# A hybrid S5 and RG-LRU layer on one core: the branch b projection in seven products per pair of blocks, and the C load in front of the S5 recurrence

## The chip, the cores and the metric

The kernel runs on one core of one Trainium2 chip. The metric is the device time of one execution in microseconds, as a median over executions. The core has a matrix engine (PE; its weight loads are listed as PEld), a vector engine (DVE), a scalar engine (ACT), GpSimd (POOL), and a sync engine (SP) which issues all DMA of this kernel.

## What is computed

One layer of a decoder trunk, for a prompt of 512 tokens and 8 sample sequences of 4 tokens, 544 tokens in all, with 2048 channels. Cut to what matters here:

```python
proj = xn @ p["w_in"] + p["b_in"]
u_a, z_a, x_b, z_b, g_a, g_b = jnp.split(proj, _SPLITS, axis=-1)
y_a, s5_re, s5_im = _s5_branch(u_a, s5_re0, s5_im0, p)
y_b, rg_h, conv_buf = _rglru_branch(x_b, rg_h0, conv0, p)
y_a = y_a * jax.nn.silu(z_a)
y_b = y_b * jax.nn.silu(z_b)
merged = (jax.nn.sigmoid(g_a) * (y_a @ p["w_proj_a"])
          + jax.nn.sigmoid(g_b) * (y_b @ p["w_proj_b"]))
out = merged @ p["w_out"]
x = x + gate[:, None] * out
```

The S5 branch is a complex diagonal recurrence h over the tokens in 64 groups of 64 states, with y = Re(C h) + D u, a GELU and a GLU. `w_proj_b` is 2048 x 2048, `w_proj_a` 1024 x 2048. All is float32.

## The kernel before

A float32 product is made of three matmuls on a rounded format: a value x is kept as hi = round(x) and lo = x - hi, and hi·xh, hi·xl and lo·xh are summed in PSUM. Activations lie with channels on the 128 partitions and tokens along the free dimension: 16 blocks of 128 channels by 544 tokens (T), two halves of 272 (HT), since a PSUM bank takes 512 values. `split_x` (176) makes xh on ACT and xl on DVE for one such block. `weights` (151) loads a raw tile of 1 MB (2048 values on each partition; three buffers) and `split_w` (137) makes hi on ACT (144) and lo on DVE (145), 1024 values each, four buffers each. `product` (165) makes one block of 128 output channels: with 16 blocks of k it issues 96 matmuls of 272 columns (line 172), with 8 blocks 48.

The stages follow one another: the ada vectors; the input projection in 80 blocks (u, z_a, the gates g_a and g_b, later x_b and z_b), beside which the S5 branch runs; the RG-LRU; the GLU of branch a (961 to 969); the a projection (974 to 984); the b projection (989 to 1000); w_out (1010 to 1063).

S5 steps are hung between the blocks of the input projection by a list, `spread` (lines 722 to 728) and `beside`: `s5_far` (powers of the transition), `s5_near`, `s5_over` and `s5_into` are the recurrence, all on DVE in `rotated` (five operations, with tiles v and t, on the state tile eh, whose neighbours along the recurrence lie eight values apart). `s5_c` loads C in four tiles r (649), transposes each on PE into q (653) and copies it by ACT to cp and cq. `s5_y1` makes ca from cp and cq and then the first matmuls of the output, pk (664). The r tiles and the recurrence's v and t share one tag with three buffers:

```python
def t2k(shape, name):
    return p1.tile(shape, F32, tag="t2k", name=name, bufs=3)
```

In the GLU, y of block j is multiplied and split into ah, al. The a projection loads gad (the gate, line 974), applies a sigmoid (976), multiplies it with the product on DVE and stores it to pad (981); beside it, ybd (the RG-LRU's output) comes back block by block and is split into bh, bl (984). The b projection loads gbd and pad, multiplies and adds on DVE (helper `tt`, line 403), and splits the merged blocks for w_out. Tiles loaded with `loaded` (800) share four buffers, tag ld.

Which instruction stands where on each engine is set by the Tile scheduler, which lays the program out by a timeline of its own; each engine then works through its list in order and waits on semaphores.

Of the kernel before, what the change touches and what calls it, by code (L numbers as in the profile page):

```python
# [9 lines left out]
F32 = mybir.dt.float32  # L10
F32R = mybir.dt.float32r
# [8 lines left out]
P = 128  # L20
# [3 lines left out]
T = TP + NS * TS  # L24
# [31 lines left out]
def tile_hybrid_s5_rglru(  # L56
# [137 lines left out]
    MC = 72  # L194
    cs = const.tile([P, KD, MC], F32R, name="cs")
    cv_ = pt[:, :KD * 9].rearrange("p (k b) -> p k b", b=9)
# [3 lines left out]

    shift = const.tile([P, KD, 9], F32, name="shift")
    gmul = const.tile([P, KD, 9], F32, name="gmul")
    gate = const.tile([P, KD, 9], F32, name="gate")
# [90 lines left out]
    def columns(pieces, name):  # L294
        t = p0.tile([P, P], F32, tag="rows", name="rows", bufs=2)
        if sum(b - a for a, b, _ in pieces) < P:
            pool.memset(t, 0.0)
        for a, b, src in pieces:
            dq2.dma_start(t[a:b], src)
        pt = aux_tile("pt")  # L300
        pe.transpose(pt[:, :P], t, ident)
        o = const.tile([P, P], F32, name=name)
        act.activation(o, pt[:, :P], AF.Copy)
        return o
# [409 lines left out]
    for q in range(16):  # L714
# [237 lines left out]

    st2.close()


# [14 lines left out]

    bh, bl = [None] * KD, [None] * KD
    for j in range(16):
        if j % 2 == 0:
            wts = weights(w_proj_a[0], j * P, 8)
        sg = loaded(gad, j, p3)
# [10 lines left out]
    mh, ml, mm = [None] * KD, [None] * KD, [None] * KD  # L986
    for j in range(16):
        sg, m_ = loaded(gbd, j, p3), p3.tile([P, T], F32, tag="mm", name="mm", bufs=8)
        dq2.dma_start(m_, pad[j])
        act.activation(sg, sg, AF.Sigmoid)  # L990
        acc = product(weights(w_proj_b[0], j * P, KD), 0, KD, bh, bl)
        for h in range(2):
            sl = slice(h * HT, (h + 1) * HT)
            tt(dve, sg[:, sl], acc[h][:, :HT], sg[:, sl], MUL)
        tt(dve, m_, m_, sg, ADD)
        mm[j] = m_
        if j < 8:
            split_x(m_, j, mh, ml)
    for j in range(8, 16):
        split_x(mm[j], j, mh, ml)  # L1000
    st3.close()
# [8 lines left out]
    for t0, t1 in ((256, T), (0, 256)):  # L1010
# [10 lines left out]
        done = 0  # L1021
        for j in range(KD):
            wts = weights(w_out[0], j * P, KD)
            acc = acc_tile("acc")
            for k in range(KD):
                h, l = wts(0, k)
                for w_, x_, first, last in ((h, mh, k == 0, False), (h, ml, False, False),
                                            (l, mh, False, k == KD - 1)):
                    pe.matmul(acc[:, :t1 - t0], lhsT=w_, rhs=x_[k][:, t0:t1], start=first, stop=last)  # L1029
            og = p4.tile([P, T - 256], F32, tag="og", name="og", bufs=3)  # L1030
            np_ = min(t1, TP) - t0
# [65 lines left out]
```

## Time and profile before

| what | us |
|---|---|
| runs, median of 3 | 1831.95 |
| lowest, highest | 1820.18, 1832.62 |
| the profiled execution | 1823.58 |
| its span in the profile | 1821.8 |
| PE busy, share of the span | 1749.4, 96% |
| DVE busy | 928.4, 51% |
| ACT busy | 737.5, 40% |

Durations come from that one profiled execution. The chain of waits is followed back from the last instruction, at each step to what released it; the share of an engine in it is time that counted. Windows give the busy time of each engine within a stretch, and the granted clock of PE (1.00 is 2.4 GHz, 0.50 is 1.2 GHz).

### The profile page before, as it was taken

Reading aid. Unit: us, or ns where it says so; the run is one execution under the profiler, and the core shown is the slowest. Engines: PE = TensorE matmul, PEld = TensorE weight load, DVE = VectorE, ACT = ScalarE, POOL = GpSimd, SP = SyncE. Lnnn points to the kernel's source line nnn. Section 1 sums busy time; section 2 is a strip of 40 time slices with the busy share of each in tenths; the row PEclk is TensorE's granted clock in tenths of the full one; section 3 lists DMA queues with packets and bytes.
Section 4 is the critical chain, followed back from the end, with each engine's and each line's share of the span. In section 5 each row is a group of like instructions: output and inputs, shape, how many; then the busy total and the mean of one; then the engine's idle time right before and its main releaser. Section 6 shows DMA issues by size and latency. Waiting matters only on the chain.

```text
span 1821.8 us, 32528 instructions
## 1 busy us (share of the span) xinstructions
PE 1749.4 (96%) x13420; PEld 1687.4 (93%) x13420; DVE 928.4 (51%) x1394; ACT 737.5 (40%) x1134; POOL 148.1 (8%) x385
## 2 busy tenths in 40 slices
PE   7889999999599999999999999999999999999997
PEld 4558999999599999999999999999999999999997
DVE  4795255548863233224556565655543433355654
ACT  7864232332122222223555545555333322134543
POOL 2100000000000000010222122321000000000000
PEclk9989999999799999999999999999999999999999
DMA  9887435442335545444444453542776644376682
GB/s 323 278 281 188 127 97 135 111 117 74 106 104 140 143 115 145 122 134 122 128 134 134 113 167 119 159 145 93 222 253 211 185 136 123 105 222 178 175 224 94
DMA packets 400278, 281.56 MB, mean 155 GB/s; under 512 B 68513, under 2 KB 350457, under 8 KB 398905
## 3 DMA queue, kind: packets, MB, share of 16 engines
q1 hardware_dynamic: 400130, 279.49, 53.1%
q8 instruction: 105, 1.72, 0.4%
q14 instruction: 43, 0.35, 0.1%
HBM read 244.64 MB, written 32.44 MB: 152 GB/s over the span
## 4 chain that ended last, share of the span: by engine, by line
PE 78%; DVE 7%; DMA 7%; ACT 4%; issue 2%; SPq 2%; POOL 0%; ACTq 0%; DVEq 0%; POOLq 0%
PE acc L172 58%; PE acc L1029 11%; DVE lo L145 2%; DMA raw<-in_w_in_dram 2%; PE pg L881 1%; DVE t L403 1%; PE gacc L821 1%; PE ada L218 1%; SPq L675 1%; DVE v L403 1%; DMA xt<-in_x_prompt_dram 1%; DMA ybd<-zb 1%; ACT hi L144 1%; PE pk L664 1%; DMA raw<-in_w_ada_dram 1%
## 5 line engine op out<-in xcount | busy, mean ns | idle before, releaser
L145 DVE TENSOR_TENSOR lo<-raw,hi 128x1024 fp32r<-128x1024 f32 x374 | 455.1, 1222 | 559.6 <-ACT hi L144 541.9
L172 PE MATMUL acc<-xh,hi 128*128 128x272 f32 x3424 | 718.2, 290 | 4.9 <-ACT adasb L228 2.6
L172 PE MATMUL acc<-xh,lo 128*128 128x272 f32 x3424 | 717.7, 289 | 1.2 <-DVE lo L145 1.2
L172 PE MATMUL acc<-xl,hi 128*128 128x272 f32 x3424 | 717.1, 289 | 0.0
L144 ACT ACTIVATE hi<-raw 128x1024 fp32r<-128x1024 f32 x374 | 391.1, 1056 | 674.3 <-PE acc L172 541.9
L172 PEld LDWEIGHTS acc<-xh,hi 128*128 128x128 f32 x3424 | 541.3, 189 | 10.8 <-ACT adasb L228 3.1
L172 PEld LDWEIGHTS acc<-xh,lo 128*128 128x128 f32 x3424 | 539.5, 189 | 2.5 <-DVE lo L145 1.7
L172 PEld LDWEIGHTS acc<-xl,hi 128*128 128x128 f32 x3424 | 540.6, 189 | 0.9 <-DVE xl L181 0.2
L1029 PE MATMUL acc<-xl,hi 128*128 128x288 f32 (+1 forms) x512 | 149.3, 292 | 0.0
L1029 PE MATMUL acc<-xh,hi 128*128 128x288 f32 (+1 forms) x512 | 148.6, 291 | 0.0
L1029 PE MATMUL acc<-xh,lo 128*128 128x288 f32 (+1 forms) x512 | 147.3, 288 | 0.0
L1029 PEld LDWEIGHTS acc<-xh,lo 128*128 128x128 f32 x512 | 96.6, 189 | 0.1
L1029 PEld LDWEIGHTS acc<-xl,hi 128*128 128x128 f32 x512 | 96.5, 188 | 0.3
L1029 PEld LDWEIGHTS acc<-xh,hi 128*128 128x128 f32 x512 | 96.2, 188 | 0.1
L403 DVE TENSOR_TENSOR ld<-acc,ld 128x272 f32<-128x272 f32 x64 | 25.2, 434 | 53.1 <-PE acc L172 53.1
L218 PE MATMUL ada<-lo,cs 128*72 128x512 f32 x128 | 45.0, 436 | 7.3 <-DVE lo L145 6.5
L218 PE MATMUL ada<-hi,cs 128*72 128x512 f32 x128 | 44.3, 430 | 7.5 <-ACT hi L144 7.1
L765 ACT ACTIVATE r<-pg,c 128x284 f32<-128x284 f32 x64 | 29.7, 492 | 39.7 <-PE pg L881 39.7
L181 DVE TENSOR_TENSOR xl<-ld,xh 128x544 fp32r<-128x544 f32 x24 | 17.3, 723 | 50.8 <-ACT xh L179 50.7
L856 DVE SCALAR_TENSOR_TENSOR cv<-xb,c,cv 128x568 f32<-128x568 f32 x48 | 38.8, 809 | 1.5
L218 PEld LDWEIGHTS ada<-hi,cs 128*72 128x72 f32 x128 | 18.6, 154 | 22.0 <-ACT hi L144 11.1
L218 PEld LDWEIGHTS ada<-lo,cs 128*72 128x72 f32 x128 | 16.7, 151 | 21.1 <-DVE lo L145 16.9
(311 smaller groups left out, 1416.2 us busy)
## 6 DMA issues: line engine op xcount, KB each, us to landing
raw<-in_w_in_dram SPq DMA_DIRECT2D x80, 1024.0 KB
raw<-in_w_ada_dram SPq DMA_DIRECT2D x64, 512.0 KB
raw<-in_w_out_dram SPq DMA_DIRECT2D x32, 1024.0 KB
raw<-in_w_ada_dram SPq DMA_DIRECT2D x16, 1024.0 KB
raw<-in_w_proj_b_dram SPq DMA_DIRECT2D x16, 1024.0 KB
raw<-in_w_proj_a_dram SPq DMA_DIRECT2D x8, 1024.0 KB
u<-ud SPq DMA_DIRECT2D x128, 41.0 KB
gad<-sg SPq DMA_DIRECT2D x16, 272.0 KB
```

The lines of the kernel that those rows point to most:

```text
L144: act.activation(hv, src, AF.Copy)
L145: dve.tensor_tensor(out=lv, in0=src, in1=hv, op=SUB)
L172: pe.matmul(acc[j][:, :HT], lhsT=w_, rhs=x_[k][:, j * HT:(j + 1) * HT], start=first, stop=last)
L218: pe.matmul(accs[i][:MC], lhsT=cs[:, k, :], rhs=w_[:, i * 512:(i + 1) * 512], start=first, stop=last)
L403: eng.tensor_tensor(out=out, in0=a, in1=b, op=op)
L664: pe.matmul(pk[:GC, i * P:(i + 1) * P], lhsT=bb[:, 4 * q + i], rhs=ca[:, i, 0:8].rearrange("p j c -> p (j c)"), start=True, stop=True)
L675: dq2.dma_start(m4[GC * (7 - s):GC * (8 - s), :, GC * s:], k4[:, :, 0:P - GC * s])
L765: turn[0] = act.activation(*args, **kw)
L821: pe.matmul(gacc[0][:MC], lhsT=cs[:, k0 + k, :], rhs=w_[:, k % 2 * 512:(k % 2 + 1) * 512], start=first, stop=last)
L856: dve.scalar_tensor_tensor(out=cv, in0=xb[:, k:k + FT], scalar=convw_c[:, k * 16 + j:k * 16 + j + 1], in1=cv, op0=MUL, op1=ADD)
L881: pe.matmul(pg[:, :FH], lhsT=w_[:, g], rhs=x_[:, sl], start=first, stop=last)
L1029: pe.matmul(acc[:, :t1 - t0], lhsT=w_, rhs=x_[k][:, t0:t1], start=first, stop=last)
```

## The change

Two parts.

The b projection takes output blocks in pairs. A weight matrix part of 2048 x 256 is cut into four quarters: even and odd blocks of k, and the first and second 128 columns (`quarters`); the activations likewise into even and odd blocks of channels and the two halves of the tokens. Strassen's scheme in Winograd's form then needs seven products of a quarter by a quarter (24 matmuls of 272 columns each) instead of eight. The seven weight operands are made one after the other by four differences on DVE, in place in the raw tiles, and split each into hi and lo (`seven_weights`). The seven activation operands a0, s1, s2, b0, s3, s4, b1 (for 8 block pairs each) are made during the a projection by `build` and `build_late`, and ybd is no longer split as it stands. Three PSUM banks a, e, b collect the products; partial results are copied by ACT and added by DVE. The merged block goes back to pad, and blocks 0 to 11 are loaded again and split during the last pair. The first two blocks of w_out are started together with k 0 to 11, and get k 12 to 15 afterwards. Constants needed only early move to a pool `early` that ends before, to make room.

The C load `s5_c` is hung in front of `s5_far`, not in the third of the four blocks that carry the recurrence.

```diff
+    def set_sums(f, a, b, eng):
+        a0, a1, b0, b1 = a[:, :HT], a[:, HT:], b[:, :HT], b[:, HT:]
+        s1, s2, s3, s4 = f
+        eng.tensor_tensor(out=s1, in0=a1, in1=b1, op=ADD)
+        eng.tensor_tensor(out=s2, in0=s1, in1=a0, op=SUB)
+        eng.tensor_tensor(out=s4, in0=b0, in1=s2, op=SUB)
+        eng.tensor_tensor(out=s3, in0=a0, in1=a1, op=SUB)
+        return {"a0": a0, "a1": a1, "b0": b0, "b1": b1, "s1": s1, "s2": s2, "s3": s3, "s4": s4}
+
+    def split_half(src, room):
+        act.activation(room[:, 0], src, AF.Copy)
+        dve.tensor_tensor(out=room[:, 1], in0=src, in1=room[:, 0], op=SUB)
+
+    def quarters(w, col):
+        out = []
+        for s in range(2):
+            raw = raw_tile()
+            dq.dma_start(raw.rearrange("p (i m) -> p i m", i=8),
+                         w[:, col:col + 256].rearrange("(i s p) m -> s p i m", s=2, p=P)[s])
+            v = raw.rearrange("p (i h m) -> p h i m", i=8, h=2)
+            out += [v[:, 0], v[:, 1]]
+        return out
+
+    ORDER = ("a0", "s1", "s2", "b0", "s3", "s4", "b1")
+
+    def seven_weights(w, col):
+        b11, b12, b21, b22 = quarters(w, col)
+        def sub(o, x, y):
+            dve.tensor_tensor(out=o, in0=x, in1=y, op=SUB)
+            return o
+        yield split_w(b11)
+        yield split_w(sub(b11, b12, b11))
+        yield split_w(sub(b11, b22, b11))
+        yield split_w(b21)
+        yield split_w(sub(b12, b22, b12))
+        yield split_w(b22)
+        yield split_w(sub(b21, b21, b11))
...
+    def seven(head, sets, left, right, bias=(None, None)):
+        g, wt = head
+        wt = wt + list(g)
+        a, e, b = (acc_tile(f"acc{x}")[:, :HT] for x in "aeb")
+        def run(n, bank, new, done):
+            for i in range(8):
+                h, l = (v[:, i * P:(i + 1) * P] for v in wt[n])
+                xh_, xl_ = sets[ORDER[n], i]
+                for w_, x_, f, z in ((h, xh_, i == 0, False), (h, xl_, False, False), (l, xh_, False, i == 7)):
+                    pe.matmul(bank, lhsT=w_, rhs=x_, start=new and f, stop=done and z, skip_group_check=True)
...
+        run(0, a, True, True)
+        run(1, e, True, True)
+        out(l0, a, bias[0])
+        out(r1, e, bias[1])
+        run(2, a, False, True)
+        out(r0, a, bias[1])
+        run(3, b, True, True)
+        dve.tensor_tensor(out=l0, in0=l0, in1=b, op=ADD)
+        run(4, a, False, True)
+        dve.tensor_tensor(out=r1, in0=r1, in1=a, op=ADD)
+        run(5, e, False, True)
+        dve.tensor_tensor(out=r0, in0=r0, in1=e, op=ADD)
+        run(6, a, False, True)
+        out(l1, a, bias[0])
...
-    spread([s5_far] + [lambda i=i: s5_near(i) for i in range(1, 8)]
+    spread([s5_c, s5_far] + [lambda i=i: s5_near(i) for i in range(1, 8)]
            + [lambda c=c, f=f: f(c) for c in range(1, 8) for f in (s5_over, s5_into)], 10, 14)
-    spread([s5_c], 12, 13)
...
+    def build(i):
+        fa = p3.tile([P, 2, HT], F32, tag="fa", name="fa")
+        fb = p3.tile([P, 2, HT], F32, tag="fb", name="fb", bufs=4)
+        v = set_sums([fa[:, 0], fa[:, 1], fb[:, 0], fb[:, 1]],
+                     loaded(ybd, 2 * i, p3), loaded(ybd, 2 * i + 1, p3), dve)
+        kept[i] = v
+        for n in ORDER if i < 4 else ORDER[:3]:
+            split_half(v[n], room[n, i])
...
-        split_x(loaded(ybd, j, p3), j, bh, bl, xpool if j < 8 else px)
...
+        if j % 2 == 0:
+            coming = weights(w_proj_a[0], (j + 2) * P, 8) if j < 14 else seven_head(w_proj_b[0], 0, 4)
+        if j in (0, 2, 4, 6, 7, 9, 11, 13):
+            build(len(kept))
+    head = coming
+    for n in ORDER[3:]:
+        build_late(n)
...
+    for j0 in range(0, 16, 2):
+        cs_ = [wk.tile([P, T], F32, tag=t_, name="c", bufs=2) for t_ in ("z", "sg")]
+        seven(head, sets, *cs_)
+        if j0 < 14:
+            head = seven_head(w_proj_b[0], (j0 + 2) * P)
+        else:
+            head = weights(w_out[0], 0, KD)
+            for j in range(12):
+                split_x(loaded(pad, j, p3), j, mh, ml)
+        for j, c in zip((j0, j0 + 1), cs_):
+            sg, m_ = loaded(gbd, j, p3), loaded(pad, j, p3)
+            act.activation(sg, sg, AF.Sigmoid)
+            tt(dve, c, c, sg, MUL)
+            tt(dve, c, c, m_, ADD)
+            merged[j] = c
+            if j < 12:
+                dq2.dma_start(pad[j], c)
+    for j in range(12, 16):
+        split_x(merged[j], j, mh, ml)
```

Where the instructions stand. Counted along PE's list, the four groups of C transposes now stand behind 2035, 2047, 2064 and 2098 matmuls of line 172, formerly behind 2499 to 2533, and the first pk behind 2623, formerly 2649. The last matmuls of `s5_e` (pw, line 569) stand behind 2027 in both.

DVE at the end of `s5_far` before, up to the recurrence's first operation v:

```order
L403 TENSOR_TENSOR q2_4037<-q1_4036,q2_4037 128x256
L403 TENSOR_TENSOR t_4060<-q2_4037,q1_4036 128x256
L145 TENSOR_TENSOR lo_4592<-raw_4585,hi_4591 128x1024
L403 TENSOR_TENSOR q1_4036<-q1_4036,t_4056 128x256
L403 TENSOR_TENSOR q2_4037<-q2_4037,t_4060 128x256
L403 TENSOR_TENSOR v_4064<-eh_1434,q1_4036 128x512
L403 TENSOR_TENSOR t_4065<-eh_1434,q2_4037 64x512 x2
```

The same place after (t_5159 is a product with cq, the transposed C):

```order
L487 TENSOR_TENSOR t_4097<-q2_4078 128x256
L487 TENSOR_TENSOR q2_4078<-q1_4077,q2_4078 128x256
L487 TENSOR_TENSOR t_4101<-q2_4078,q1_4077 128x256
L487 TENSOR_TENSOR t_5159<-a2_1439,cq_4058 128x576
L487 TENSOR_TENSOR q1_4077<-q1_4077,t_4097 128x256
L487 TENSOR_TENSOR q2_4078<-q2_4078,t_4101 128x256
L487 TENSOR_TENSOR v_4105<-eh_1437,q1_4077 128x512
```

The first product with cq has moved in front of the recurrence, and the t tiles take buffers that the r tiles of C had just before.

ACT at the change from the GLU (line 965 before, 1049 after) to the a projection before; ld of line 976 is the gate gad, xh of line 179 the split of y:

```order
L144 ACTIVATE hi_14043<-raw_14037 128x1024
L965 ACTIVATE sg_13894<-acc0_13844,c1_224 128x272
L965 ACTIVATE sg_13894<-acc1_13845,c1_224 128x272
L976 ACTIVATE ld_13975<-ld_13975 128x544
L179 ACTIVATE xh_13899<-ld_13840 128x544
L179 ACTIVATE xh_13971<-ld_13969 128x544
L144 ACTIVATE hi_14173<-raw_14171 128x1024
```

The same place after; xset are the operands of `build(0)`, fa holds s1 and s2, fb s3 and s4, ld_14025 and ld_14027 are ybd blocks:

```order
L146 ACTIVATE hi_14019<-raw_14013 128x1024
L1049 ACTIVATE sg_13898<-acc0_13848,c1_227 128x272
L1049 ACTIVATE sg_13898<-acc1_13849,c1_227 128x272
L198 ACTIVATE xset_13907<-fa_14023 128x272
L198 ACTIVATE xset_13911<-fa_14023 128x272
L198 ACTIVATE xset_13915<-ld_14027 128x272
L198 ACTIVATE xset_13919<-fb_14024 128x272
L181 ACTIVATE xh_13903<-ld_13844 128x544
L198 ACTIVATE xset_13923<-fb_14024 128x272
L198 ACTIVATE xset_13927<-ld_14027 128x272
L198 ACTIVATE xset_13931<-ld_14025 128x272
```

The last split of y (xh_13903, before xh_13899) now stands behind four copies of build(0), and the gate's sigmoid behind it.

DVE in the b projection before, one block of 128 channels and part of the next:

```order
L403 TENSOR_TENSOR mm_15125<-mm_15125,ld_15123 128x544
L145 TENSOR_TENSOR lo_15375<-raw_15368,hi_15374 128x1024
L181 TENSOR_TENSOR xl_15241<-mm_15125,xh_15239 128x544
L145 TENSOR_TENSOR lo_15491<-raw_15488,hi_15490 128x1024
L403 TENSOR_TENSOR ld_15243<-acc0_15258,ld_15243 128x272
L403 TENSOR_TENSOR ld_15243<-acc1_15259,ld_15243 128x272
L403 TENSOR_TENSOR mm_15245<-mm_15245,ld_15243 128x544
```

DVE there after, most of one pair; line 219 is a difference of weights, line 262 and 264 (not in this piece) the additions from PSUM:

```order
L487 TENSOR_TENSOR c_15653<-c_15653,ld_15876 128x544
L147 TENSOR_TENSOR lo_15865<-raw_15855,hi_15864 128x1024
L487 TENSOR_TENSOR c_15653<-c_15653,ld_15878 128x544
L219 TENSOR_TENSOR raw_15855<-raw_15857,raw_15855 128x8x128
L147 TENSOR_TENSOR lo_15888<-raw_15855,hi_15887 128x1024
L147 TENSOR_TENSOR lo_15892<-raw_15857,hi_15891 128x1024
L487 TENSOR_TENSOR c_15652<-c_15652,ld_15868 128x544
L147 TENSOR_TENSOR lo_15897<-raw_15855,hi_15896 128x1024
L219 TENSOR_TENSOR raw_15857<-raw_15857,raw_15855 128x8x128
L487 TENSOR_TENSOR c_15652<-c_15652,ld_15870 128x544
L147 TENSOR_TENSOR lo_15901<-raw_15857,hi_15900 128x1024
L147 TENSOR_TENSOR lo_15906<-raw_15857,hi_15905 128x1024
```

The differences stand between the lo of the products, in the order in which the seven products need them.

## Rows read from the trace of the kernel before

**Rows 1.** The page: busy time, and the chain by line.
```profile
PE 1749.4 (96%) x13420; PEld 1687.4 (93%) x13420; DVE 928.4 (51%) x1394; ACT 737.5 (40%) x1134; POOL 148.1 (8%) x385
...
PE acc L172 58%; PE acc L1029 11%; DVE lo L145 2%; DMA raw<-in_w_in_dram 2%; PE pg L881 1%; DVE t L403 1%; PE gacc L821 1%; PE ada L218 1%; SPq L675 1%; DVE v L403 1%; DMA xt<-in_x_prompt_dram 1%; DMA ybd<-zb 1%; ACT hi L144 1%; PE pk L664 1%; DMA raw<-in_w_ada_dram 1%
```

**Rows 2.** Windows: length, busy PE, PEld, DVE, ACT, POOL, clock, DMA share, GB/s.
```profile
1330.00:1418.00 88.00, 88.00 (x699) 88.00 (x698) 33.09 (x53) 30.68 (x45) 0.00 (x0) 1.00 0.72 223
1415.00:1608.00 193.00, 193.00 (x1526) 193.00 (x1525) 74.19 (x99) 55.35 (x66) 0.00 (x0) 1.00 0.47 131
1608.00:1640.00 32.00, 32.00 (x245) 31.88 (x245) 15.02 (x26) 11.66 (x14) 0.15 (x2) 1.00 0.92 286
```

**Rows 3.** Waits: engine, line, releaser, us in total, times, longest.
```profile
PE q L653 <- DMA r<-in_s_c_im_dram: 18.4, 1, 18.4
...
PE acc L172 <- ACT xh L179: 2.3, 1, 2.3
...
DVE v L403 <- PE q L653: 6.7, 1, 6.7
...
DVE t L403 <- PE q L653: 1.8, 1, 1.8
```

**Rows 4.** Chain of waits: start, us, what; from three stretches.
```profile
417.99 12.08 PE acc L172 x96
...
1279.80 8.27 DMA raw<-in_w_proj_a_dram
...
1318.11 2.76 DMA ld<-gad
...
1320.97 0.66 ACT ld L976
1321.63 0.55 ACT xh L179
...
1322.23 24.29 PE acc L172 x190
```

**Rows 5.** Lines by form, DVE and ACT in 1420:1600; the last row DVE in 1322:1414.
```profile
L145 DVE TENSOR_TENSOR lo<-raw,hi 128x1024 fp32r<-128x1024 f32 x31 | 37.8, 1222 | 68.1 <-ACT hi L144 68.1
L403 DVE TENSOR_TENSOR ld<-acc,ld 128x272 f32<-128x272 f32 x31 | 12.2, 435 | 45.7 <-PE acc L172 45.7
L403 DVE TENSOR_TENSOR mm<-mm,ld 128x544 f32<-128x544 f32 x15 | 10.9, 726 | 0.6
...
L144 ACT ACTIVATE hi<-raw 128x1024 fp32r<-128x1024 f32 x31 | 32.5, 1056 | 79.5 <-PE acc L172 79.5
...
L145 DVE TENSOR_TENSOR lo<-raw,hi 128x1024 fp32r<-128x1024 f32 x13 | 15.8, 1219 | 7.2 <-ACT hi L144 7.2
```

**Rows 6.** Lines by form, DVE in the S5 recurrence, 419:521.
```profile
L145 DVE TENSOR_TENSOR lo<-raw,hi 128x1024 fp32r<-128x1024 f32 x12 | 14.5, 1218 | 0.1
...
L403 DVE TENSOR_TENSOR v<-eh,q 128x512 f32<-128x512 f32 x7 | 8.2, 1167 | 0.2
```

**Rows 7.** Windows of 2 us, in the ada stage and before the a projection.
```profile
106.00:108.00 2.00, 0.00 (x0) 0.00 (x0) 1.85 (x3) 1.66 (x4) 0.00 (x0) 0.53 1.08 344
...
114.00:116.00 2.00, 2.00 (x10) 2.00 (x10) 1.60 (x7) 2.00 (x4) 0.00 (x0) 0.50 0.24 67
...
1320.00:1322.00 2.00, 0.00 (x0) 0.00 (x0) 0.17 (x1) 1.03 (x2) 0.00 (x0) 1.00 0.54 147
```

**Rows 8.** Windows of 4 us, behind the wait at the C transposes.
```profile
498.00:502.00 4.00, 4.00 (x20) 4.00 (x19) 0.80 (x1) 1.38 (x2) 0.00 (x0) 0.50 0.66 167
...
506.00:510.00 4.00, 4.00 (x35) 4.00 (x34) 3.91 (x10) 1.54 (x2) 0.00 (x0) 1.00 0.09 23
```

**Rows 9.** Timeline of DVE at 419; chain of waits at 492 and 521.
```profile
419.18 1.16 DVE L403 TENSOR_TENSOR v<-eh,q 128x512 f32<-128x512 f32 x1
...
492.85 4.43 DMA r<-in_s_c_im_dram
...
521.02 0.68 DVE ca L403
```

More of the change, by code (lines that the diff above doesn't have):

```diff
@@ L71, in tile_hybrid_s5_rglru @@
     const = ctx.enter_context(tc.tile_pool(name="const", bufs=1))
+    ste = ExitStack()
+    early = ste.enter_context(tc.tile_pool(name="early", bufs=1, side="right", reuse_waits="tile"))
     wpool = ctx.enter_context(tc.tile_pool(name="wpool", bufs=4))
@@ new lines, in seven_head, with out @@
+    def seven_head(w, col, n=2):
+        g = seven_weights(w, col)
+        return g, [next(g) for _ in range(n)]
+    def seven(head, sets, left, right, bias=(None, None)):
[8 more added lines that the diff above has]
+                    pe.matmul(bank, lhsT=w_, rhs=x_, start=new and f, stop=done and z, skip_group_check=True)
+        def out(dst, bank, bias_):
+            if bias_ is None:
+                act.activation(dst, bank, AF.Copy)
+            else:
+                act.activation(dst, bank, AF.Identity, bias=bias_)
+        l0, l1, r0, r1 = left[:, :HT], left[:, HT:], right[:, :HT], right[:, HT:]
+        run(0, a, True, True)
[12 more added lines that the diff above has]
+        out(l1, a, bias[0])
@@ L301, in columns @@
         pe.transpose(pt[:, :P], t, ident)
-        o = const.tile([P, P], F32, name=name)
+        o = (const if name == "c1" else early).tile([P, P], F32, name=name)
         act.activation(o, pt[:, :P], AF.Copy)
@@ L969, in tile_hybrid_s5_rglru, with rooms, build_late @@
         split_x(y_, j, ah, al)
-    bh, bl = [None] * KD, [None] * KD
+    sets = {}
+    def rooms(pl, n, *keys):
+        for key in keys:
+            t = pl.tile([P, 2, HT], F32R, tag="xs", name="xset", bufs=n)
+            sets[key] = t[:, 0], t[:, 1]
+            room[key] = t
+    room = {}
+    rooms(px, 16, *((n, i) for n in ("s1", "s2", "b0", "s3") for i in range(4)))
+    rooms(p3, 8, *((n, i) for n in ("s4", "b1") for i in range(4)))
+    rooms(xpool, 32, *(("a0", i) for i in range(8)), *((n, i) for n in ORDER[1:3] for i in range(4, 8)))
+    kept = {}
+    def build(i):
[6 more added lines that the diff above has]
+            split_half(v[n], room[n, i])
+    def build_late(n):
+        for i in range(4, 8):
+            h = {"b0": 0, "b1": 1}.get(n)
+            src = kept[i][n]
+            if h is not None:
+                src = loaded(ybd, 2 * i + 1, p3)[:, h * HT:(h + 1) * HT]
+            split_half(src, room[n, i])
+    coming = weights(w_proj_a[0], 0, 8)
     for j in range(16):
         if j % 2 == 0:
-            wts = weights(w_proj_a[0], j * P, 8)
+            wts, coming = coming, None
         sg = loaded(gad, j, p3)
@@ L983, in tile_hybrid_s5_rglru @@
             rows_out((j - 4) * P)
-        split_x(loaded(ybd, j, p3), j, bh, bl, xpool if j < 8 else px)
[L986 to L1000, printed above, removed]
+        if j % 2 == 0:
+            coming = weights(w_proj_a[0], (j + 2) * P, 8) if j < 14 else seven_head(w_proj_b[0], 0, 4)
+        if j in (0, 2, 4, 6, 7, 9, 11, 13):
+            build(len(kept))
+    rooms(xpool, 32, *((n, i) for n in ORDER[3:] for i in range(4, 8)))
+    head = coming
+    for n in ORDER[3:]:
+        build_late(n)
+    mh, ml = [None] * KD, [None] * KD
+    merged = {}
+    for j0 in range(0, 16, 2):
[3 more added lines that the diff above has]
+            head = seven_head(w_proj_b[0], (j0 + 2) * P)
+        else:
+            head = weights(w_out[0], 0, KD)
[11 more added lines that the diff above has]
+        split_x(merged[j], j, mh, ml)
     st3.close()
@@ L1021, in tile_hybrid_s5_rglru, with block @@
         done = 0
[L1022 to L1025, printed above, removed]
+        def block(acc, wts, k0, k1):
+            for k in range(k0, k1):
                 h, l = wts(0, k)
@@ L1029, in tile_hybrid_s5_rglru @@
                     pe.matmul(acc[:, :t1 - t0], lhsT=w_, rhs=x_[k][:, t0:t1], start=first, stop=last)
+        begun = []
+        if t0:
+            begun = [(acc_tile("acc"), w_) for w_ in (head, weights(w_out[0], P, KD))]
+            for k0, k1 in ((0, 12), (12, KD)):
+                for b_ in begun:
+                    block(*b_, k0, k1)
+        for j in range(KD):
+            if j < len(begun):
+                acc = begun[j][0]
+            else:
+                acc = acc_tile("acc")
+                block(acc, weights(w_out[0], j * P, KD), 0, KD)
             og = p4.tile([P, T - 256], F32, tag="og", name="og", bufs=3)
```

7 lines of the change are left out of this document (4 added, 3 removed).

## The prediction, made before the result was known

> **What bounds the kernel now.** I read the busy shares first, then the waits of TensorE (PE), then the stages by windows, then the chain of waits at the two places that the change touches, and last the durations by form. PE is busy for 1749.4 of 1821.8 us and the products of line 172 are 58% of the chain that ended last [rows 1]: a removed matmul counts in full unless something else fills its place. In the b projection (1415 to 1608) PE is busy for all 193.00 us, DVE for 74.19, ACT for 55.35; in the a projection PE for 88.00 of 88.00, DVE 33.09 [rows 2]. PE's two waits that matter here are 18.4 us in the S5 recurrence, at the transposes of C, and 2.3 us between GLU and a projection [rows 3].
>
> The profiled execution took 1823.58 us, 1.8 more than its span. The sum below is made against it. The median of the three runs, 1831.95, is 8.4 us above it, and their spread is 12.4 us: 1% (18.3 us) is about what a measurement of this kernel can tell from no change.
>
> **1. Fewer matmuls in the b projection.** Before: 16 blocks of 96. After: 8 pairs of seven products of 24, that is 168, 1344 in all, so 192 fewer, each still 272 columns wide. 96 such matmuls took 12.08 us [rows 4], 0.1258 each, and 1536 of them make 193.2, the stage's length. Saved: 192 x 0.1258 = **24.2 us**, if PE stays the bound. A pair then lasts 168 x 0.1258 = 21.1 us.
>
> Does it stay the bound? DVE per pair: 7 lo and 4 weight differences of 1024 elements at 1.222 us (13.4), 3 additions from PSUM at 0.435 (1.3), 4 operations of 544 at 0.726 (2.9) [rows 5]: 17.6 of 21.1 us, 83% against 38% before. ACT has seven hi of 1.056 us and six smaller ones, about 11. The differences are the new form: their sources are runs of 128 out of every 256 values. The nearest rows are the lo of the a projection, which reads the same kind of halves, at 1219 ns, and the recurrence's v<-eh, whose source lies eight values apart, at 1167 for 512 elements, or 2.28 ns an element [rows 5, 6]. I take the first; the second is a rival below. With 83% the order still has to fit: the four lo buffers feed 4 x 24 matmuls, 12.1 us of PE. Walking one pair in its order, the tightest place is the second raw tile of the next pair. It is issued only when the differences of the pair have freed a buffer, about 7.5 us into the pair, and is needed at about 15.6. A raw load with the same rows of 256 columns took 8.27 us [rows 4], so it is just in time. I cost it at nothing, with 0 to 1 us a pair as its bounds.
>
> The Trainium skill ("SBUF — State Buffer", Door 1: The DMA port swizzle) says that SBUF serves 16-byte lines and that a stride which leaves less than two hits in a line pays a penalty. By it the differences, with their long runs, cost what lo costs and v<-eh is slow because of its stride; by the penalty's reading they would be the 2.3 us of the rival. [Rows 5, 6] agree with it as far as they go, and the sum does not need it.
>
> **2. The change from GLU to a projection.** Before, PE's last wait there ended with gad's load (issued 1318.11, landed 1320.87), ACT's sigmoid and its xh, and PE resumed at 1322.23 [rows 4]. In the new order ACT's last xh stands behind four copies of the operands of build(0), and two of these are of sums that need the second ybd tile. That load takes the slot at 1318.11 that gad had, so it lands near 1320.9. From there on DVE: s1 (0.43), one lo (1.22), s2 (0.43), so 1322.95; then ACT copies s2, a0, s3 at about 0.45 each (half the width of a 0.66 copy gives 0.33 to 0.66), 1324.4, and xh, 1325.0. DVE's xl comes about half a microsecond later behind five more operations. PE resumes 2.8 to 3.3 us later: **+3**. A wait that long has a second price. Early in the program PE did nothing from 106 to 108, the granted clock was 0.53 there, and it was still 0.50 at 114 to 116; in the shorter gap at 1320 it stayed at 1.00 [rows 7]. After the recurrence's wait PE did 20 matmuls in 4 us at clock 0.50 where 35 go at full speed [rows 8]. A gap of more than 5 us will, I expect, look like the first: about 4 us at the 1.2 GHz level, half of it lost, **+2**. Together +5 (bounds 0, if the second ybd tile comes as early as gad did without one, and +8).
>
> **3. The rest of the a projection.** The builds give DVE at most eleven operations of half width (0.43 each, 4.7 us) for every two blocks, 12.1 us of PE, and take the two xl away; it had 33.09 of 88 busy [rows 2]. So it stays below PE: 0. The four late b0 at the start of the b projection: 0 to 1, within part 1's tolerance.
>
> **4. C loads in front of the recurrence.** The transposes move to before the recurrence; the PE wait of 18.4 us and DVE's 6.7 and 1.8 us on them go [rows 3]. What is late next is DVE itself: it was the chain through the whole recurrence, from v at 419.18 to ca, ready at 521.70, and only 8.5 us of these 102.5 were idle [rows 3, 9]. The r tiles and the recurrence's t and v tiles share three buffers (tag t2k). So in the new order the first t of s5_far waits for the second C transposes, about 421.3 (20 matmuls and two groups of transposes behind 417.99), and its last t's for the third ones, near 424.0; then DVE has some 3.5 us to do before the first v, with t<-a,cq among it: **v starts near 428**, 8.8 later. Against that: 8.5 of idle gone, two lo fewer inside (10 where 12 stood [rows 6], -2.4), t<-a,cq already done (-0.7). ca is ready at 419.18 + 8.8 + 102.5 - 8.5 - 2.4 - 0.7 = 518.9, or 2.8 earlier. But the first pk matmul now stands behind 2623 products instead of 2649: 26 x 0.1258 = 3.3 us more work is left behind the same wait. And the wait has only moved: between 418 and 518.9 PE has 596 products, 75.0 us, and some 2 us of transposes, so it idles for about 24 us, nearly all in front of pk, and comes back at clock 0.50 on the path [rows 8], while before that slow stretch lay in front of the pk wait where it was covered: +2.2. In sum -2.8 + 3.3 + 2.2 = **+3**. Bounds: all of the wait regained (-18.4) and, if far starts later still because the r loads, one of which took 4.43 us [rows 9], come late behind the loads of u, +8. I take +3 since DVE's row is the nearest.
>
> **5. Last pair and w_out.** Twelve merged tiles come back from memory to be split, four at a time through the ld slots, while the differences of the last pair run. By hand, the last xl is ready 38 us after the last pair's start and is needed at 40.6, since the first two w_out blocks begin with k 0 to 11. DMA must move 5.9 MB in 21 us, 280 GB/s; the same place shows 286 in 1608 to 1640 [rows 2]. At the limit of what the rows show: **+1** (0 to 6).
>
> Sum: -24.2 + 5 + 3 + 1 = -15.2, so 1823.6 - 15.2 = **1808.4 us**.
>
> **Rivals.**
> A. PE's wait for C is regained: -18.4 instead of +3 gives 1787. For it speaks that PE's wait is named after the r load; against it that DVE in that stretch is busy whenever it isn't waiting for these very transposes [rows 3, 9].
> B. DVE binds the b projection: with 2.28 ns an element the four differences cost 2.33 each, 9.3 instead of 4.9, and DVE needs 22.0 us a pair plus its waits, say 22.5: 180 us instead of 169. That is 11 on top, 1819.5. For it: the v<-eh row; against: the lo row on halves.
> C. The slower side: the second raw tile of each pair comes late. Its time from issue to landing is L; PE waits L - 8.1 in each of eight pairs. At L = 11.1 that is 24 us and the saving is gone; at 12.5 it is 35, and 1808.4 + 35 = 1843.4. For it: two loads each of gbd and pad and two stores beside the 2 MB of weights, some 3.7 MB in 21.1 us or 175 GB/s, where the stage had 131; and 8.27 was already seen. Against: other stretches carry 223 and 286 GB/s without a wait of PE [rows 2].
> D. The saving does not show because the scheduler's pieces around it (transition, last pair, late operands) each take their upper bound: +8, +8 and +6 instead of 5, 3 and 1 give 1821.4.
>
> **How the numbers follow.** Forecast 0.56 (own range 1800 to 1818), A 0.13, B 0.10, C 0.11, D 0.10. Faster by over 1% means below 1805.2 on this scale: A, and half of the forecast's case, since its terms of +5, +3 and +1 can each fall out at nothing: 0.13 + 0.28 = 0.41. Slower by over 1%, above 1841.9, needs C with L of 12.3 or more, the most of its chance: 0.10. The rest, 0.49, is within 1%. The range leaves out half of A and most of C's upper end: 1787 to 1832.
>
> **What would show it.** Right: b stage about 169 us with PE full and DVE near 83%; difference rows near 1.22 us; PE's wait at q gone and one of about 20 us at pk, with clock 0.50 behind it; a gap of 5 us before the a projection. Wrong: a wait of PE for lo or hi in each pair (B if DVE is full, C if the wait behind it ends with a raw load); ca ready before 512; PE idle for over 4 us in front of w_out.

## The result, and the profile after

The changed kernel took 1813.28 us (median of 8 executions, 1807.7 to 1818.57) where the kernel before took 1826.25 (8 executions, 1820.18 to 1832.62): a ratio of 0.9924, with a 95% interval of 0.9905 to 0.9944. That is 13 us, 0.76%, within the 1% that the forecast called no change; the forecast was 15.2 us. Beside three other kernels it gave 1811.66 against 1828.22, 0.9909 (0.9886 to 0.9932).

Its profiled execution happened to be the longest of the eight (1818.57 us, span 1816.8). The second profile, of the same program, took 1811.72, near the median; where one number is needed, both are given.

The page of the changed kernel, to be held against [rows 1]: its busy times and its chain by line. Line 174 is the old line 172, line 244 the seven products.

```profile
PE 1731.7 (95%) x13228; PEld 1667.3 (92%) x13228; DVE 1022.8 (56%) x1530; ACT 779.2 (43%) x1230; POOL 150.3 (8%) x385
...
PE acc L174 44%; PE acc L1158 11%; PE acca L244 5%; DVE lo L147 2%; PE acce L244 2%; DMA raw<-in_w_in_dram 2%; DVE t L487 2%; DMA ld<-ybd 2%; DVE v L487 2%; PE pg L964 1%; PE ada L302 1%; PE gacc L904 1%; PE accb L244 1%; DMA pad<-ld 1%; DMA xt<-in_x_prompt_dram 1%
```

192 matmuls fewer (13228 against 13420). DMA ld<-ybd and pad<-ld are new among the entries shown: loads and stores that go through the four ld slots.

Five of PE's longer waits in the changed kernel, over the whole program, to be held against [rows 3] ("..." stands for two in the ada stage):

```profile
PE pk L748 <- DVE ca L487: 18.0, 1, 18.0
...
PE accb L244 <- ACT hi L146: 6.5, 1, 6.5
PE acc L174 <- DVE lo L147: 4.8, 4, 1.9
PE py L771 <- DMA m<-k: 4.4, 2, 2.4
PE acc L174 <- ACT xh L181: 3.9, 2, 3.6
```

The 18.4 us at the transposes became 18.0 at pk, and a wait of 6.5 us at the first product with b0 (accb) is new.

Windows of the changed kernel: the steady part of the b projection, and the two stalls. Columns as in [rows 2].

```profile
1330.00:1332.00 2.00, 1.26 (x7) 1.26 (x8) 2.00 (x7) 1.65 (x5) 0.00 (x0) 0.78 0.90 268
1332.00:1334.00 2.00, 2.00 (x11) 2.00 (x11) 1.12 (x4) 0.00 (x0) 0.00 (x0) 0.50 1.03 318
1334.00:1336.00 2.00, 2.00 (x15) 2.00 (x15) 0.79 (x2) 0.99 (x2) 0.00 (x0) 0.86 0.92 321
1430.00:1432.00 2.00, 0.00 (x0) 0.00 (x0) 1.00 (x3) 0.00 (x0) 0.00 (x0) 1.00 0.36 81
1434.00:1436.00 2.00, 0.00 (x0) 0.00 (x0) 2.00 (x6) 1.82 (x4) 0.00 (x0) 0.50 0.43 135
1438.00:1440.00 2.00, 2.00 (x11) 2.00 (x11) 2.00 (x5) 2.00 (x6) 0.00 (x0) 0.50 0.56 189
1440.00:1600.00 160.00, 158.90 (x1263) 158.46 (x1263) 129.33 (x145) 76.62 (x108) 0.00 (x0) 1.00 0.62 188
```

From 1440 to 1600 PE is busy for 158.90 of 160 us with DVE at 129.33, 81%: the seven products run at PE's pace. In front of it PE stands idle from 1429.7 to 1436.25, and the clock is still 0.50 at 1438 to 1440.

The time between marks that both programs pass in the same order (start times of the last pw, the second pk, the last gacc of the RG-LRU, PE's first product after the wait in front of the a projection, and the last product of w_out), read from timelines and tile views:

| stretch | before | changed | changed, second profile |
|---|---|---|---|
| start to last pw | 417.7 | 417.2 | 415.1 |
| to second pk (recurrence) | 110.4 | 112.2 | 112.0 |
| to last gacc | 735.9 | 740.1 | 735.0 |
| to the a projection | 58.2 | 61.2 | 61.4 |
| to the last product of w_out | 486.8 | 473.3 | 473.6 |

The third row is the same work in all three. Its spread of 5 us is no effect of the change, since the second profile of the same changed program has 735.0: in the first, two waits for m were longer (4.4 us together, against 1.7 in the second) and the clock fell behind them. The mark that parts the last two rows stands seven matmuls later in the changed kernel (446 matmuls behind the last gacc instead of 439, counted in the traces). So 0.9 us of the fourth row's increase is work that the fifth row lost.

### The profile page after: what moved, and what is told of

Its sections match the earlier page's. It is cut to its first block, busy times and chain, and to the rows that moved or that the text cites. A ratio compares the mean times of both kernels' runs of the same rounds, so it can differ in the third digit from the quotient of the medians.

```text
span 1816.8 us, 32529 instructions
## 1 busy us (share of the span) xinstructions
PE 1731.7 (95%) x13228; PEld 1667.3 (92%) x13228; DVE 1022.8 (56%) x1530; ACT 779.2 (43%) x1230; POOL 150.3 (8%) x385
## 4 chain that ended last, share of the span: by engine, by line
PE 72%; DMA 10%; DVE 9%; ACT 3%; issue 3%; SPq 2%; POOL 0%; ACTq 0%; DVEq 0%; POOLq 0%
PE acc L174 44%; PE acc L1158 11%; PE acca L244 5%; DVE lo L147 2%; PE acce L244 2%; DMA raw<-in_w_in_dram 2%; DVE t L487 2%; DMA ld<-ybd 2%; DVE v L487 2%; PE pg L964 1%; PE ada L302 1%; PE gacc L904 1%; PE accb L244 1%; DMA pad<-ld 1%; DMA xt<-in_x_prompt_dram 1%
## 5 line engine op out<-in xcount | busy, mean ns | idle before, releaser
L174 PE MATMUL acc<-xh,hi 128*128 128x272 f32 x2912 | 614.0, 291 | 6.7 <-ACT xh L181 3.9
L174 PE MATMUL acc<-xh,lo 128*128 128x272 f32 x2912 | 612.7, 290 | 4.8 <-DVE lo L147 4.8
L174 PE MATMUL acc<-xl,hi 128*128 128x272 f32 x2912 | 611.2, 290 | 0.2 <-DVE xl L183 0.2
L174 PEld LDWEIGHTS acc<-xh,hi 128*128 128x128 f32 x2912 | 461.8, 189 | 12.8 <-ACT xh L181 4.3
L174 PEld LDWEIGHTS acc<-xh,lo 128*128 128x128 f32 x2912 | 460.1, 189 | 6.5 <-DVE lo L147 5.7
L174 PEld LDWEIGHTS acc<-xl,hi 128*128 128x128 f32 x2912 | 461.1, 190 | 1.2 <-DVE xl L183 0.5
L244 PE MATMUL acca<-xset,hi 128*128 128x272 f32 x512 | 96.8, 288 | 0.0
L1158 PEld LDWEIGHTS acc<-xh,lo 128*128 128x128 f32 x512 | 96.6, 189 | 0.1
L1158 PEld LDWEIGHTS acc<-xl,hi 128*128 128x128 f32 x512 | 96.5, 188 | 0.2
L1158 PEld LDWEIGHTS acc<-xh,hi 128*128 128x128 f32 x512 | 96.0, 188 | 0.1
L244 PEld LDWEIGHTS acca<-xset,hi 128*128 128x128 f32 x512 | 80.1, 188 | 0.0
L244 PE MATMUL acca<-xset,lo 128*128 128x272 f32 x256 | 72.9, 288 | 0.0
L244 PE MATMUL acce<-xset,hi 128*128 128x272 f32 x256 | 49.6, 288 | 0.4 <-ACT hi L146 0.4
```

The costliest lines, as they stand in the source:

```text
L174: pe.matmul(acc[j][:, :HT], lhsT=w_, rhs=x_[k][:, j * HT:(j + 1) * HT], start=first, stop=last)
L244: pe.matmul(bank, lhsT=w_, rhs=x_, start=new and f, stop=done and z, skip_group_check=True)
```

## The experiments

**The two parts alone.** `c_back` is the changed kernel with the C load back where it was; `c_front` is the kernel before with the C load in front.

```diff
-    spread([s5_c, s5_far] + [lambda i=i: s5_near(i) for i in range(1, 8)]
+    spread([s5_far] + [lambda i=i: s5_near(i) for i in range(1, 8)]
...
+    spread([s5_c], 12, 13)
```

> The changed kernel with the C load back in the third block of the recurrence; the b projection by seven products stays. Theory (the C move only shifts PE's wait from the transposes to pk and costs about 2 to 3 us, since DVE's recurrence sets the end): 2 to 3 us below the changed kernel, 1810 to 1811.5 where it has 1813.3; PE waits 18 us at the transposes again and 1 to 2 us at pk, the second pk starts about 2 us earlier relative to the last pw. Rival (the move regains the wait and the b projection gives little): 10 to 18 us above the changed kernel.

> The kernel before with nothing changed but the C load put in front of the recurrence. Theory: 2 to 3 us slower than before, PE's wait of 18.4 us at the transposes gone and one of about 18 us at pk in its place, v of the recurrence starting near 427.5. Rival (the wait is regained): 10 to 18 us faster than before. A second rival (the later stalls at py behind the SP queue of 630 to 700 come with the move): 5 to 7 us slower than before.

`c_back` gave 0.9900 of before (0.9883 to 0.9917), so the b projection alone carries the gain, about 18 us (15 to 21 by the interval, from four executions). That it is faster than the changed kernel is not shown, since the intervals overlap. PE waits 18.9 us at the transposes again and 1.6 at pk, as its theory said. `c_front` gave 0.9981 (0.9968 to 0.9994), a little faster, where the theory said slower. Its profile has what the theory said: PE waits 16.5 us at pk instead of 18.4 at the transposes, and from the last pw to the second pk (start to start) pass 112.6 us, not 110.4. But that execution was the longest of its twelve, with a start that took 7 us more. So it was run once more.

> The kernel before with the C load alone in front of the recurrence, a second time, since its first 12 runs came out 0.998 of before while its profile showed 2.0 us more between the last pw and the second pk, and two pairs of kernels with the seven products put the move at 2 to 4 us slower. If the first result was chance of the program's start (the last pw ends anywhere from 415 to 426 us in the profiles, with the same program up to there): 1.000 to 1.002 of before, and again 112 us and not 110 between the last pw and the second pk. If the move really saves time somewhere else: 0.998 again, and the stretch from the second pk to the first gacc shorter than before's 329.7 us by more than 4 us.

0.9994 (0.9977 to 1.0012), 111.3 us between the two marks, and 330.5 us from the second pk to the first gacc, where before has 329.7. The first alternative holds, as 1.000 lies within the interval and the second asked for a shorter stretch behind: the move costs 1 to 2 us in its place and nothing measurable in the time. All fourteen profiles of this case agree on the place: from the last pw to the second pk pass 110.2 to 111.0 us in the five kernels with the C load in the third block, and 111.3 to 113.2 in the nine with it in front. In no run did the move regain the wait.

The chain of waits in the changed kernel shows why, in the order of [rows 9]; start, length, what:

```profile
420.41 0.44 PE q L737 x4
...
425.01 0.42 DVE t L487
...
427.44 1.04 DVE v L487
...
517.05 0.77 DVE ca L487
517.82 0.14 issue
517.95 1.87 PE pk L748 x8
```

v starts at 427.44 (forecast: near 428). What holds the s5_far in front of it is its first t tile, which has to wait for a buffer of r and so for the second group of transposes (420.41 above); the last column says what the idle time before waited for:

```profile
420.89 0.22 DVE L487 TENSOR_TENSOR t<-q 128x64 f32<-128x64 f32 x1 [3.59 <-PE q L737]
```

From v on DVE runs on, with one wait of 0.3 us, to ca at 517.82 (forecast: 518.9). Counted from the last pw, ca is ready 3.3 us earlier than before (100.7 us against 104.0), but 67 matmuls instead of 41 stand between the first and the second pk, 3.3 us more, and PE has nothing left from about 500 and comes back at the 1.2 GHz level, which costs the remaining 2 us:

```profile
502.00:505.00 3.00, 0.00 (x0) 0.00 (x0) 2.94 (x5) 0.00 (x0) 0.00 (x0) 1.00 0.00 0
...
517.00:520.00 3.00, 2.05 (x9) 1.29 (x10) 2.97 (x5) 0.14 (x1) 0.53 (x1) 0.50 0.00 0
520.00:523.00 3.00, 3.00 (x17) 3.00 (x18) 2.67 (x6) 0.44 (x1) 0.00 (x0) 0.64 0.50 142
```

**The wait at the first b0 product, first try.** `b0_late` changes the order of the seven products, so that the reloaded b0 comes sixth.

```diff
-    ORDER = ("a0", "s1", "s2", "b0", "s3", "s4", "b1")
+    ORDER = ("a0", "s1", "s2", "s3", "s4", "b0", "b1")
```

> The changed kernel with the seven products in another order: a0, s1, s2, s3, s4, b0, b1, so that the operand that is loaded again (b0) is needed 48 matmuls (6 us) later and the two that lie ready come first. Theory (the 6.5 us wait of PE at the first b0 product, and the 3.6 us at half clock behind it, are the term that the forecast missed): 6 to 8.5 us below the changed kernel, 1805 to 1807.5, with no wait of PE over 2 us between 1425 and 1445. Rival (the wait is due to ACT and DVE being full there, whatever the order): the wait reappears at s3 or b0 and the time stays within 2 us.

0.9984 (0.9969 to 0.9999), some 11 us worse than the changed kernel: the theory fails, and the rival's "within 2 us" as well. PE waits 10.1 us for ACT's copy of bank a, since in front of that copy ACT stands at late tiles as before. Line 198 is the copy of an operand, 248 that of a bank; the last column is again what the idle time before waited for:

```profile
1427.18 0.43 ACT L198 ACTIVATE xset<-ld 128x272 fp32r<-128x272 f32 x1 [1.75 <-DMA ld<-ybd]
1428.55 0.43 ACT L198 ACTIVATE xset<-ld 128x272 fp32r<-128x272 f32 x1 [0.94 <-DMA ld<-ybd]
1428.88 1.04 ACT L146 ACTIVATE hi<-raw 128x1024 fp32r<-128x1024 f32 x1
1429.83 0.38 ACT L248 ACTIVATE c<-acca 128x272 f32<-128x272 f32 x1
```

The order also brings five waits of bank a for lo, 3.5 us together, in the later pairs. So putting b0 later does not help while ACT's queue is as full. The test is not a clean one: with the new order the fourth product adds to bank a, whose copy it must wait for, where in the changed kernel it goes to the free bank b. Part of the 10.1 us may be due to that.

**The changed kernel again, and the loads taken out of the ld slots.** In the changed kernel itself the fourth weight's hi stands on ACT behind copies that wait for ybd:

```profile
1428.95 0.74 ACT L198 ACTIVATE xset<-ld 128x272 fp32r<-128x272 f32 x2
1433.49 0.43 ACT L198 ACTIVATE xset<-ld 128x272 fp32r<-128x272 f32 x1 [3.80 <-DMA ld<-ybd]
1434.18 0.43 ACT L198 ACTIVATE xset<-ld 128x272 fp32r<-128x272 f32 x1 [0.26 <-DMA ld<-ybd]
1434.52 0.73 ACT L198 ACTIVATE xset<-fb 128x272 fp32r<-128x272 f32 x2
1435.15 1.04 ACT L146 ACTIVATE hi<-raw 128x1024 fp32r<-128x1024 f32 x1
```

These loads are issued only from 1430.68 on. On SP they stand behind the store of the last but one a block (issued at 1428.66; the last one's follows at 1435.12), and they take the slots of earlier late tiles when DVE has made their lo (line 199). In the chain of waits, where the second of these loads is the one that counted:

```profile
1430.22 0.78 DVE xset L199 x2
...
1431.09 3.00 DMA ld<-ybd
```

`late_wk` loads the late b0 through two other tags, idle at that time, half as wide:

```diff
-                src = loaded(ybd, 2 * i + 1, p3)[:, h * HT:(h + 1) * HT]
+                src = wk.tile([P, T], F32, tag=("z", "sg")[i % 2], name="lb", bufs=2)[:, :HT]
+                dq2.dma_start(src, ybd[2 * i + 1][:, :HT])
```

> The changed kernel once more, with nothing edited, as the base for the three kernels beside it on the same chip, and for a second profile of it. If the stalls are the program's own: the waits at pk (18 us), in front of the a projection (3 to 4 us) and at the first b0 product (6 to 7 us) stand again with the clock at half behind each; if the waits at py between 640 and 720 are chance, they differ from the first profile's 4.4 us with clock 0.96. Time 0.992 to 0.993 of before.

> The changed kernel with the late b0 operands loaded into the z and sg buffers that are idle in the a projection, half as wide, and not through the four ld slots. Theory (at the start of the b projection ACT stands in order at copies of late b0 tiles whose loads can only be issued when an ld slot is freed by the last pad store; the next weights' hi stands behind them): PE's 6.5 us wait at the first b0 product falls to 2 us or less and the clock stays at 1.00, 6 to 8.5 us below the changed kernel. Rival (ACT and DVE simply have too much to do there): wait and time stay within 2 us.

`after_again`: 0.9909; the wait at b0 was 6.4 us, at pk 16.5, in front of the a projection 3.6; at py 1.7 us. So the first three belong to the program and the length of the fourth is chance. `late_wk`: 0.9923 (0.9901 to 0.9946), no faster. The wait on the load is gone, but the scheduler filled ACT with late copies, 14 of them (1422.4 to 1426.9), in front of the same hi, and PE waited 3.1 us for hi and 2.1 for lo, 5.2 instead of 6.4. (The slots of the two loads that ACT waited for were freed, as shown above, not by the last pad store, as the theory has it, but by DVE.)

**Those copies moved to GpSimd.** `late_pool` adds to `late_wk`:

```diff
-            split_half(src, room[n, i])
+            if n == "b0":
+                split_half(src, room[n, i])
+            else:
+                pool.tensor_copy(room[n, i][:, 0], src)
+                pool.tensor_tensor(out=room[n, i][:, 1], in0=src, in1=room[n, i][:, 0], op=SUB)
```

> The changed kernel with the late b0 tiles loaded through the z and sg buffers as in late_wk, and with the copies and differences for the late s3, s4 and b1 on GpSimd, which is idle there. In late_wk 14 half-width copies still stood on ACT in front of the fourth weight's hi (1422.4 to 1426.9). Theory (in-order ACT, filled with late copies, is what delays hi and so the first b0 product): with only four copies in front of it, PE's wait there falls from 5 to 6.5 us to 2 us or less, at full clock, and the time lies 5 to 8 us below the changed kernel, near 0.988 of before. Rival (the wait has another cause, such as the hi buffers or GpSimd's own pace of some 0.7 us an operation, 24 of them): PE then waits as long at s3 or b1, and the time stays within 2 us of the changed kernel.

> The same with the C load back in the third block of the recurrence. Seven profiles put the C move at +2.0 us between the last pw and the second pk; the runs of it alone came out 3.5 us faster than before. Theory (the move costs 2 us and nothing else): 2 us below late_pool. Rival (the move saves some 3 us that the profiles do not show): 3 us above late_pool.

`late_pool`: 0.9923 (0.9899 to 0.9947). ACT now reaches the hi in time:

```profile
1422.07 1.06 ACT L146 ACTIVATE hi<-raw 128x1024 fp32r<-128x1024 f32 x1 [2.91 <-DVE raw L219]
1423.04 1.37 ACT L198 ACTIVATE xset<-lb 128x272 fp32r<-128x272 f32 x4
1424.32 1.99 ACT L146 ACTIVATE hi<-raw 128x1024 fp32r<-128x1024 f32 x2
```

and PE's waits at b0 are 1.4 us for hi and 2.5 for DVE's lo, 3.9 instead of 6.4; the clock fell all the same behind them. The theory had 2 us or less at full clock. That ACT's queue held the hi is shown, its price in the time is not. At b0's place 3.9 us of idle remain and some 6 us of work at the half clock, half of it lost: about 7 of the 8.5 us. PE now waits mostly for DVE, which is busy for all 4.00 us from 1424 to 1428.

The profiles and the medians part here. From the first product of the a projection to the last of w_out `late_pool` takes 468.0 us in its profile and `late_pool_cback` 465.5, against 473.3 and 473.6 in the changed kernel. (About 1.5 us of `late_pool`'s gain is the clock in front of the a projection, which did not fall in that execution; `late_pool_cback` has 3.0 us of wait at b0 and the clock stays at 1.00 there.) The medians do not have this gain: 1814.74 us is not below the changed kernel's 1813.28 and 1811.66, and the intervals would hide one of a few us. In the `late_pool` kernels the time is 2.2 to 2.5 us above the span, 1.8 in the others, which is 0.4 to 0.7 us of it; the rest is open. `late_pool_cback`: 0.9900 (0.9876 to 0.9923), 1810.86 us, 3.9 below `late_pool`. Like `c_back` it points to a small cost of the C move in this kernel, but the intervals overlap.

**The gap in front of the a projection.** `build_later` hangs the builds behind odd blocks; `first_wk` loads the first build's two ybd tiles through the z tag.

```diff
-        if j in (0, 2, 4, 6, 7, 9, 11, 13):
+        if j in (1, 3, 5, 6, 8, 10, 12, 13):
```

> The changed kernel with each of the builds hung behind an odd block of the a projection (1, 3, 5, 6, 8, 10, 12, 13), so that none stands in front of the last split of the GLU's y. Theory (the first build's sums on the late ybd tile hold ACT's last split by 3 us, and the longer gap drops the clock for 3.4 us): PE's gap before the a projection falls back to about 2.5 us at full clock, 4 to 5 us below the changed kernel, 1808 to 1809.5, unless the later builds lengthen the wait at b0. Rival (the gap is set by the loads' queue on SP, not by the build's place): the gap stays at 4 us or more and the time within 1.5 us.

> The changed kernel with the two ybd tiles of the first build loaded into the z buffers during the GLU and not through the ld slots. Theory (the second ybd tile of the first build, late for want of an ld slot, holds ACT's last split of y): PE's wait in front of the a projection falls from 3.6 us to 2 us or less, without the half clock behind it, 3 to 5 us below the changed kernel. Rival (the gate loads, which now stand ahead, hold it as they did in the kernel before): the wait stays at 2 to 4 us, time within 2 us.

`build_later`: 0.9957 (0.9942 to 0.9973), some 8 us slower than the changed kernel, so neither alternative holds. The gap stayed at 3.7 us: a ybd load stands in the chain in front of the last xh here too (issued at 1318.73, PE resumes at 1324.39). The start of the b projection now waits 4.7 us for the last a block and 4.1 at b0. `first_wk`: 0.9935 (0.9913 to 0.9958). Its gap is 2.3 us, what it was before, and set by the same thing as in [rows 4], a gate load without a slot:

```profile
1322.39 2.74 DMA ld<-gad
...
1325.21 0.66 ACT ld L1101
1325.87 0.55 ACT xh L181
...
1326.47 13.65 PE acc L174 x94
```

The clock fell behind this gap all the same (0.67 and 0.50 in the windows from 1326 to 1330). Time gained: none that can be measured. The wait is as the rival had it.

**All together.** `best2` has `c_back`, `late_wk` and `first_wk`; `late_pool_first` has GpSimd's share as well.

> Both of these edits, and the C load back in the third block of the recurrence. Theory: the savings add up, 11 to 16 us below the changed kernel, near 0.984 of before (24 us of matmuls and almost no new wait). Rival (each stall removed only uncovers the next one, in the ld slots): no more than 5 us below the changed kernel.

> The kernel late_pool_cback with the first build's ybd tiles loaded into the z buffers during the GLU, as in first_wk. Theory: PE's wait in front of the a projection goes from 3.6 to 2.3 us, which with less half clock behind it gives 2 to 3 us more; fastest of all, 0.983 to 0.987 of before. Rival (first_wk was no faster, since the gate loads hold ACT there instead): within 1.5 us of late_pool_cback.

0.9915 (0.9894 to 0.9936) and 0.9898 (0.9874 to 0.9922). For both the rival holds: `best2` is 1 us or less from the changed kernel, not 11 to 16 below, and `late_pool_first` is 1.2 us below `late_pool_cback`, not 2 to 3. The second, 1809.64 us, has the lowest median, with `c_back` (1810.01) beside it. It beats the kernel before clearly; that it beats the changed kernel is not shown, since the intervals overlap.

## Why the prediction was right

**Matmuls, -24.2: right.** The steady part goes at 158.90 of 160 us. The differences took what the lo did and not 2.3 us; lines by form, DVE in 1440:1590 of the changed kernel:

```profile
L147 DVE TENSOR_TENSOR lo<-raw,hi 128x1024 fp32r<-128x1024 f32 x50 | 60.8, 1221 | 22.1 <-ACT hi L146 22.1
L219 DVE TENSOR_TENSOR raw<-raw 128x1024 f32<-128x1024 f32 x28 | 34.2, 1221 | 1.7 <-DMA raw<-in_w_proj_b_dram 1.3
```

That decides against rival B. Rival C had its place right, a raw load that comes just in time, but DVE waited for one only 1.3 us in seven pairs. By the Trainium skill ("SBUF — State Buffer", Door 1: The DMA port swizzle) consecutive accesses to the same 16-byte line run at full bandwidth. The trace agrees: the differences, with runs of 128 values, took 1221 ns like the lo.

**GLU to a projection, +5: right chain, too large.** The chain went as forecast; in the profile of the changed kernel:

```profile
1324.41 2.67 DMA ld<-ybd
...
1327.47 1.22 DVE lo L147
1328.68 0.36 DVE fa L192
1329.07 1.07 ACT xset L198 x3
1330.14 0.56 ACT xh L181
1330.74 24.92 PE acc L174 x183
```

From the issue of the load that counts to PE's first product it takes 6.33 us (6.29 in the second profile) against 4.12 in [rows 4]: 2.2 us more, where the forecast had 2.8 to 3.3. The table's 3.0 and 3.2 include the 0.9 us of seven matmuls that changed sides of the mark. The gap itself was 3.65 us, not 5. The +2 for the clock was there too (0.78, 0.50, 0.86 in the windows from 1330) and cost 1.5: the first 190 products took 25.6 us instead of 24.1. But it is no sure difference. `c_front`, whose engines work through the same list there as before's, has the old gap of 2.3 us and then

```profile
1328.00:1330.00 2.00, 0.10 (x1) 0.00 (x0) 0.28 (x1) 0.90 (x2) 0.00 (x0) 1.00 0.66 158
1330.00:1332.00 2.00, 1.65 (x7) 1.65 (x8) 1.36 (x2) 0.85 (x2) 0.00 (x0) 0.55 1.06 373
1332.00:1334.00 2.00, 2.00 (x12) 2.00 (x11) 0.90 (x3) 1.06 (x1) 0.00 (x0) 0.60 0.99 325
```

where [rows 7] had 1.00, and its first 190 products took 25.6 us too. So that list pays it too in some executions; the single profile of before was taken for a rule.

**Start of the b projection, 0 to 1: wrong, the step that failed.** It cost 6.5 us of wait (6.4 in the second profile) and about 2 us of half clock behind it. The forecast asked when PE would need the late b0 and whether DVE had time; it did not ask what ACT, which works in order, would have standing in front of the next hi, nor when the ld slots would let the b0 loads be issued.

**C in front, +3: right in kind, and +1.7 in size** (112.2 and 112.0 against 110.4). The three parts of the sum came out near: -3.3 (forecast -2.8), +3.3 and about +2 (forecast +2.2). PE waited 18.0 us at pk, not "about 24". Rival A falls: the wait moved from the transposes to pk.

**Last pair and w_out, +1: 0.** PE goes from accb and acce straight into line 1158 (w_out, from 1599.8 on) without a wait of its own, and DMA carries more than the 280 GB/s that the forecast asked for:

```profile
1600.00:1620.00 20.00, 20.00 (x155) 20.00 (x154) 15.14 (x21) 11.44 (x17) 0.15 (x2) 1.00 1.06 301
1620.00:1640.00 20.00, 20.00 (x154) 19.70 (x154) 12.04 (x26) 9.27 (x17) 0.00 (x0) 1.00 1.06 340
```

Added up from the profiles, the terms are -24.2 + 8.5 (b0) + 2.2 (GLU to a projection) + 1.5 (the clock there, which the profile of before was spared) + 1.7 (C), and small waits of lo in the b projection, about 1: -9. The table without its first and third rows gives -8.7 and -8.4. The medians say -13 to -17. Part of the rest is known: the profiled execution of before is 2.7 us below its median and had no half clock in front of the a projection. The start up to the last pw, the same program everywhere, ended between 415.1 and 425.9 us in the fourteen profiles, which makes single profiles a poor measure of the whole. What else parts them stays open; it is there without the C move too, since `c_back` has a wait of 6.3 us at b0 in its profile and yet a median 18 us below before.

So the mechanism was right in four of its five parts, but that 13 us lies so near to 15.2 is partly luck. The sum missed some 9 us in one place (b0, with the small waits), counted 3 to 4 us too much in the others, and was made against one execution of before that was faster than its median.

## What to carry to other kernels

Here the matmuls that were removed from a stage that PE bounds were saved in full, and what went wrong lay at the seams between stages. So price the seams, and at each one list what stands ahead of the first needed operation on every in-order engine, and which buffer its load waits for. A wait that is named after a transfer was not regained by an earlier transfer, since another engine was full through the same stretch: the wait moved to that engine's result. Taking one cause of the seam at b0 away showed the next (load, then copies, then lo), each worth less than the run-to-run spread.

## What the runs showed of the hardware that was not expected

Whether PE's clock falls behind a short gap differs between executions, and between 2.2 and 3.7 us the length of the gap does not tell. In front of the a projection the clock stayed at 1.00 behind gaps of 2.3 us (before) and 3.3 us (`late_pool`, `b0_late`), and the next 190 products took 24.1 us. In the other eleven profiles it fell, behind 2.25 us in `c_front`, whose engines work through the same list there as before's, and they took 25.6 to 27.2 us. The windows of `late_pool`:

```profile
1324.00:1326.00 2.00, 0.00 (x0) 0.00 (x0) 2.00 (x4) 0.94 (x4) 0.00 (x0) 1.00 0.00 0
1326.00:1328.00 2.00, 1.02 (x8) 1.02 (x9) 2.00 (x6) 1.89 (x6) 0.00 (x0) 1.00 0.85 238
```

The spread of the times goes with the mean granted clock. The 62 executions of before that ran beside the experiments lie between 1820.95 us at 0.985 and 1836.44 us at 0.978 (correlation -0.86, some 1.5 us for 0.001). The profiled execution had 0.984, their median is 0.982.

GpSimd took 693 ns for a copy of 272 values and 1159 ns for a difference (its spans are rough in these profiles), against about 0.35 to 0.43 us on ACT and DVE:

```profile
L1094 POOL TENSOR_TENSOR xset<-fb,xset 128x272 fp32r<-128x272 f32 x8 | 9.1, 1159 | 0.0
...
L1093 POOL CAST xset<-fb 128x272 fp32r<-128x272 f32 x7 | 4.7, 693 | 0.0
```
